# A hybrid decoder layer on one core: where squares, features and the last rows of a projection stand at a block change

## The chip, the cores and the metric

The kernel runs on one core of one Trainium2 chip. The metric is the device time of one execution in microseconds. Three executions of the kernel before gave 3461.42, 3449.73 and 3450.88 us, so the median is 3450.88 us. A lower time is better.

## What is computed

The reference is one layer of a decoder step, in float32. It takes a prompt of 2048 tokens (one sequence) and 8 x 8 sample tokens with a cache, 1024 channels wide.

```python
h = rmsnorm(x, norm_mix) * (1 + sc_m) + sh_m
proj = h @ w_in                      # 1024 x 3584: rq rk rv rg sq sk sv
ro = retention(rotary(rq), rotary(rk), rv)          # 4 heads, group norm, times silu(rg)
so = stick_breaking_attention(sq, sk, sv)           # 8 heads, causal, rms norm per head
x = x + g_m * (concat(ro, so) @ w_out)
h = rmsnorm(x, norm_ffn) * (1 + sc_f) + sh_f
a, b = h @ w_up_gate, h @ w_up_val   # 1024 x 2816 each
ff = (silu(causal_conv3(a)) * b) @ w_down
x = x + g_f * ff
y = rmsnorm(x, norm_final)
```

Scales, shifts and gates (`sc`, `sh`, `g`) come from a small product of the condition with `w_ada`. The outputs are `y` for prompt and sample, and the new keys, values, retention states and convolution states.

## The kernel before

**Precision.** Every large product is made of three matmuls: both operands are split into a high part (a rounded copy on ScalarE, L174) and a low part (the difference, on VectorE or GpSimd, L159), and high x high, high x low and low x high add up in one PSUM bank (`mm3`, L295 to L297). L159, L174 and L165 are lines of small helpers that record all element-wise operations, all splits and all DMAs, so in the profile one tells them apart by the names of the tiles.

**Tiles.** The prompt is cut into four blocks of 512 tokens (`g` = 0 to 3), each of four tiles of 128 tokens. The 64 sample tokens ride as a fifth tile with block 0 of the input projection and with block 3 of the output projection and the MLP. The features of the current block, the normalised and modulated rows turned so that channels lie across partitions, stand in two buffers `act0` and `act1` (channels 0 to 511 and 512 to 1023, high and low part). There is one set of them, so features of the next block overwrite those of the current one.

**How features are made.** Rows of a tile are squared on ScalarE with a running sum, GpSimd turns the sum into a factor (`rows_rstd`: add, scale, power), the rows are scaled by it, and `to_features` (L427) does the rest by halves: four transposes on TensorE into one `z` bank of PSUM (L401), modulation by two operations on VectorE for the first half of the channels or four on ScalarE (L413) for the second, the high part on ScalarE (L424), and the low part on VectorE or GpSimd.

**The input projection (`in_block`, L608).** For a block it computes the columns of `w_in` group by group: queries and keys with channels across partitions (weights stationary, `dense_pair`, `dense_fm`), and values and gate with tokens across partitions (`token_major`, L661: features stationary, four PSUM banks `d`, one per tile, a loop over eight k of 128 channels in pairs). In `token_major` the order is k by k over the tiles; only the last pair runs tile by tile (`by_tile`). After the loop come the weights of the next block's first columns (`next_weights`, loads and both splits), then `fin` for each tile, which empties its bank (`fin_rg`: sigmoid, two products, a store). RG is the last group in blocks 0 to 2. Ahead of it `look_ahead` loads and normalises the first three row tiles of the next block. The next block begins with `to_features` of all four tiles; the fourth is loaded and normalised there.

**Output projection and MLP.** `out_block` (L1205) adds the output projection to the rows in two halves of 512 columns. After the first half, tile by tile: a product with the gate on VectorE out of the PSUM bank into a buffer `hf`, an addition on GpSimd (`residual`), a square on ScalarE (L1240). After the second half, tile by tile: `residual`, square (L1243), factor, the scaling of both halves (L1245 and L1246). Then `to_features` for all tiles. `ffn_block` (L1269) runs over the 22 column tiles of the MLP in four parts (`PARTS`); each part computes gate and value columns, then adds its piece of the down product in two halves. In the last part, after the first half, come the residual, a square (L1390) and a product with the final norm's weights on GpSimd, tile by tile. Between the first and the second half of the last part the whole `out_block` of the next 512 tokens is run (`yield from after`), features included, and then the down product's second half, tile by tile, with the final norm (`finish`, L1347) behind it. The first gate columns of the next block are loaded and split just ahead of those residuals.

**What sets the order.** Each stage is a Python generator that yields an estimate of its TensorE time. `_weave` always advances the stream that is furthest behind its share, so input projection, decoding of the sample, retention and attention, and later the MLP and attention, alternate piece by piece. The source order that results is not yet that of the engines: the compiler plans each engine's queue by its own estimates, takes the source order as priority, and picks what it expects to be ready. On the chip each engine then runs its queue in order. Buffers are counted by tag: three `hf` in both phases, three `c` and two `a` for MLP blocks, six `whl` for split weights (a pair is one weight tile's high and low part), four `d` and three `z` banks in PSUM.

## Time and profile before

| | |
|---|---|
| median of three executions | 3450.88 us |
| the profiled execution's own time | 3453.42 us |
| its span, first to last instruction | 3451.7 us |
| mean granted TensorE clock | 0.982 |
| busy: TensorE / VectorE / ScalarE / GpSimd | 95% / 66% / 52% / 30% |
| DMA | 527.71 MB, 153 GB/s |

PE is the matrix engine (TensorE), PEld its weight loads, DVE VectorE, ACT ScalarE, POOL GpSimd, SP the engine whose queue issues the DMAs. Lines of a view name engine, source line, operation, the tiles as out<-in without buffer numbers, and times in microseconds or, for a mean of one, nanoseconds; a wait in brackets is the engine's idle time before an instruction and what ended it. PEclk is the share of the full clock that TensorE was granted. Input blocks 1, 2 and 3 begin at about 328, 627 and 914 us; features for the four MLP blocks are made from about 1285, 1850, 2430 and 2984 us; attention ends at 2885 us.

### The profile page before, as it was taken

To read this page: it belongs to the slowest core of one execution; us is meant where nothing else is said; L and a number is where in the kernel's file an instruction comes from. 1 tells how busy PE (TensorE), PEld (TensorE's weight loads), DVE (VectorE), ACT (ScalarE), POOL (GpSimd) and SP (SyncE) were. 2 spreads that over 40 slices of the span, in tenths; PEclk is the share of its full clock that TensorE was granted. 3 is DMA by queue.
4 is the path that set the end of the run, shared out by engine and by line. 5 is a ranking of instruction groups with operands and counts; after the bars stand their busy time and mean duration, and the time that the engine had idled before them with its cause. 6 is when DMAs were issued, how large, how long until landed. Compare 5 with 4: busy or idle time off the path is not lost. (4 is left out here: it accounts for less than half of the span.)

```text
span 3451.7 us, 49588 instructions
## 1 busy us (share of the span) xinstructions
PE 3287.4 (95%) x17111; PEld 2683.8 (78%) x17111; DVE 2288.9 (66%) x3258; ACT 1779.6 (52%) x3153; POOL 1018.7 (30%) x1898
## 2 busy tenths in 40 slices
PE   7998999999999989999998999999899999999998
PEld 5877777776677767877877788777677787799997
DVE  5466666665555567777777787876877775554545
ACT  5457566654544446555556555554655553433223
POOL 3012011101343233434334343333433323321113
PEclk8999999999999999999999999999999999999999
DMA  6766766666756773433454343335333334332221
GB/s 227 232 200 193 231 224 224 220 229 201 212 172 197 242 215 107 123 115 120 122 185 130 107 124 112 118 109 189 110 119 107 115 103 138 119 110 84 80 86 65
DMA packets 406232, 527.71 MB, mean 153 GB/s; under 512 B 27830, under 2 KB 244009, under 8 KB 405982
## 3 DMA queue, kind: packets, MB, share of 16 engines
q1 hardware_dynamic: 405982, 524.55, 48.4%
q8 instruction: 136, 2.23, 0.3%
q14 instruction: 114, 0.93, 0.1%
HBM read 442.47 MB, written 81.99 MB: 152 GB/s over the span
## 5 line engine op out<-in xcount | busy, mean ns | idle before, releaser
L159 DVE TENSOR_TENSOR whl<-raw,whl 128x1024 fp32r<-128x1024 f32 x456 | 572.9, 1260 | 557.5 <-ACT whl L174 552.2
L174 ACT CAST whl<-raw 128x1024 fp32r<-128x1024 f32 x456 | 477.1, 1050 | 901.7 <-PE d L296 636.4
L295 PE MATMUL d<-act,whl 128*128 128x512 f32 (+2 forms) x2016 | 740.3, 368 | 7.8 <-ACT act L424 7.0
L297 PE MATMUL d<-act,whl 128*128 128x512 f32 (+2 forms) x2016 | 736.0, 365 | 4.6 <-DVE whl L159 4.6
L296 PE MATMUL d<-act,whl 128*128 128x512 f32 (+2 forms) x2016 | 733.1, 364 | 3.1 <-POOL act L159 2.2
L295 PEld LDWEIGHTS d<-act,whl 128*128 128x128 f32 x2016 | 384.6, 191 | 67.9 <-ACT act L424 8.7
L297 PEld LDWEIGHTS d<-act,whl 128*128 128x128 f32 x2016 | 384.2, 191 | 64.8 <-DVE whl L159 5.9
L296 PEld LDWEIGHTS d<-act,whl 128*128 128x128 f32 x2016 | 385.4, 191 | 59.8 <-POOL act L159 2.6
L295 PE MATMUL d<-whl,ff 128*128 128x512 f32 x704 | 280.2, 398 | 0.0
L297 PE MATMUL d<-whl,ff 128*128 128x512 f32 x704 | 279.4, 397 | 0.0
L296 PE MATMUL d<-whl,ff 128*128 128x512 f32 x704 | 279.1, 396 | 0.0
L295 PE MATMUL d<-whl,act 128*128 128x512 f32 x640 | 258.0, 407 | 10.4 <-DVE hf L159 9.3
L296 PE MATMUL d<-whl,act 128*128 128x512 f32 x640 | 258.3, 404 | 0.1
L297 PE MATMUL d<-whl,act 128*128 128x512 f32 x640 | 257.1, 402 | 0.0
L1139 DVE TENSOR_TENSOR_SCAN aom<-aom,acy 128x512 f32<-128x512 f32 x192 | 251.6, 1310 | 3.6 <-ACT aom L1125 3.0
L159 DVE TENSOR_TENSOR abe<-abe,aom 128x512 f32<-128x512 f32 (+2 forms) x320 | 232.1, 725 | 27.0 <-POOL abe L1129 5.1
L1163 PE MATMUL acc<-ahl,avv 128*128 128x512 f32 (+3 forms) x640 | 226.4, 413 | 17.6 <-ACT ahl L174 9.9
L1125 ACT ACTIVATE aom<-z,nb 128x512 f32<-128x512 f32 (+2 forms) x320 | 201.4, 629 | 74.6 <-PE z L1122 58.1
L1122 PE MATMUL z<-akk,aq 128*128 128x512 f32 (+3 forms) x640 | 192.9, 377 | 12.0 <-DVE scd L159 5.8
L1126 ACT ACTIVATE abe<-z,bb 128x512 f32<-128x512 f32 (+2 forms) x320 | 200.1, 625 | 0.0
L159 DVE TENSOR_TENSOR ahl<-z,ahl 128x512 fp32r<-128x512 f32 (+1 forms) x320 | 191.4, 598 | 6.7 <-ACT ahl L174 6.4
L159 POOL TENSOR_TENSOR ff<-ff,hf 128x512 f32<-128x512 f32 (+1 forms) x101 | 159.4, 1600 | 105.3 <-DVE hf L159 91.5
(292 smaller groups left out, 6208.8 us busy)
## 6 DMA issues: line engine op xcount, KB each, us to landing
raw<-in_w_in SPq DMA_DIRECT2D x56, 1024.0 KB
raw<-in_w_up_gate SPq DMA_DIRECT2D x44, 1024.0 KB
raw<-in_w_up_val SPq DMA_DIRECT2D x44, 1024.0 KB
akk<-k SPq DMA_DIRECT2D x160, 256.0 KB
page<-in_cache_k_pages SPq DMA_DIRECT2D x128, 256.0 KB
page<-in_cache_v_pages SPq DMA_DIRECT2D x128, 256.0 KB
raw<-in_w_down SPq DMA_DIRECT2D x32, 1024.0 KB
raw<-in_w_ada SPq DMA_DIRECT2D x24, 1024.0 KB
```

The source lines that it names most:

```text
L159: eng.tensor_tensor(o, a, b, op)
L174: act.copy(hi, src)
L295: pe.matmul(ps, sh, mh, start=start, stop=False)
L296: pe.matmul(ps, sh, ml, start=False, stop=False)
L297: pe.matmul(ps, sl, mh, start=False, stop=stop)
L1122: pe.matmul(z[:, :n], qs[g, h][:, i * P : (i + 1) * P], kk[:, c, :n], start=c == 0, stop=c == 1)
L1125: act.activation(om[:, :n], z[:, :n], AF.Sigmoid, bias=nb[:, h : h + 1], scale=-SCALE)
L1126: act.activation(be[:, :n], z[:, :n], AF.Sigmoid, bias=bb[:, h : h + 1], scale=SCALE)
L1139: dve.tensor_tensor_scan(rv, rv, rv, init, ALU.mult, ALU.bypass)
L1163: pe.matmul(accs[0][:, cs], kv[u][1][:, kt, :], m[:, cs], start=(s == g and kt == 0 and c == 0), stop=(s == 0 and kt == NT - 1 and c == 1),)
```

## The change

It has two parts, both about the order of work where a block gives way to the next.

The MLP's part. A list `later` holds work that is to be put into the program some steps on; `tick` counts it down. In `out_block` the squares of the first half go in after two weight pairs of the second half, and in `ffn_block` the square and the product with the final norm's weights go in after the first weight pair of the next `out_block` (at once in the last block). The squares of the second half write their throw-away output to `hf` and follow all four residuals. `out_block` no longer makes the features; it returns a generator `features` that scales rows two tiles ahead. `ffn_block` takes one step of it ahead of the second half of the down product and one behind each tile's matmuls. For the first MLP block all of it runs at once, as before.

The input projection's part. In blocks 0 to 2 the RG columns go through `last_rows`: the first four k as before, the last four tile by tile, and behind each tile its `fin` and the features of the same tile of the next block. The first split of the next block's weights is put ahead of these tiles, the second behind them. `look_ahead` fetches all four row tiles, the fourth into a buffer of the tag `st`. The features at the start of a block and `next_weights` are gone.

```diff
     def in_rows(g, ip, i):
-        x = T(ip, [P, D], F32, "vst" if i == 2 else "xt")
+        x = T(ip, [P, D], F32, ("xt", "xt", "vst", "st")[i])
...
-        if g:
-            for i, o, n in tiles:
-                to_features(ahead.pop((g, i), None) or in_rows(g, ip, i), o, n, coef[0], coef[1], acts, ip)
...
+        def last_rows(col, fin):
+
+            pss = [pd() if i < NT else pz() for i, _, _ in tiles]
+            ws, nxt = [], None
+            for k0, (hi, lo) in w_tm(w_in, 0, KT, col):
+                if k0 >= KT - 4:
+                    ws.append((k0, hi, lo))
+                    continue
+                for k in range(k0, k0 + 2):
+                    for tile in tiles:
+                        tok_mm(
+                            pss[tile[0]], act_rows(k, tile, smp), (hi[:, k - k0, :], lo[:, k - k0, :]),
+                            k == 0, False,
+                        )
+                yield cost / 2
+            key = RQ if g + 1 == NB - 1 else SQ
+            nxt = w_fm(w_in, key)
+            first_in[g + 1, 0, key] = [next(nxt)]
+            for tile in tiles:
+                i, o, n = tile
+                for k0, hi, lo in ws:
+                    for k in range(k0, k0 + 2):
+                        tok_mm(
+                            pss[i], act_rows(k, tile, smp), (hi[:, k - k0, :], lo[:, k - k0, :]),
+                            False, k == KT - 1,
+                        )
+                fin(i, n, fold(pss[i], n, ip))
+                if i < NT:
+                    to_features(ahead.pop((g + 1, i)), o, n, coef[0], coef[1], acts, ip)
+                yield cost / len(tiles)
+            first_in[g + 1, 0, key] += list(nxt)
...
         def look_ahead():
-            if g + 1 < NB:
-                for i in range(3):
-                    ahead[(g + 1, i)] = in_rows(g + 1, ip, i)
+            for i in range(NT):
+                ahead[(g + 1, i)] = in_rows(g + 1, ip, i)
...
-            yield from token_major(RG, fin_rg, next_weights if g < NB - 1 else None)
+                yield from last_rows(RG, fin_rg)
+            else:
+                yield from token_major(RG, fin_rg)
...
+    later = []
+
+    def tick(n=1):
+
+        for e in later:
+            e[0] -= n
+        while later and later[0][0] <= 0:
+            later.pop(0)[1]()
...
+        def squares(i, half):
+            n = tiles[i][2]
+            junk = T(fp, [P, 512], F32, "hf")
+            act.activation(
+                junk[:n], x2[i][:n, half * 512 : half * 512 + 512], AF.Square, accum_out=ss[i][:n, half : half + 1]
+            )
...
                 yield cost / 2
-            cs = slice(half * 512, half * 512 + 512)
+                tick()
             for i, o, n in tiles:
                 residual(pss[i], gates[half][i == NT], x2[i], half, n, fp, dve if half else pool)
                 if half == 0:
-                    junk = T(fp, [P, 512], F32, "hf")
-                    act.activation(junk[:n], x2[i][:n, cs], AF.Square, accum_out=ss[i][:n, 0:1])
-                else:
-                    xa, xb = T(fp, [P, 512], F32, "c"), T(fp, [P, 512], F32, "a")
-                    act.activation(xa[:n], x2[i][:n, cs], AF.Square, accum_out=ss[i][:n, 1:2])
-                    r = rows_rstd(ss[i], n)
-                    act.activation(xa[:n], x2[i][:n, :512], AF.Copy, scale=r[:n, 0:1])
-                    dve.tensor_scalar(xb[:n], x2[i][:n, 512:], r[:n, 0:1], None, ALU.mult)
-                    xn.append((xa, xb))
+                    later.append([2, lambda i=i: squares(i, 0)])
+        tick(9)
+        rs = []
         for i, o, n in tiles:
-            to_features(xn[i], o, n, coef[2], coef[3], acts, fp)
-            yield 1.0
-        return x2
+            squares(i, 1)
+            rs.append(rows_rstd(ss[i], n))
+
+        def features():
+            xn = {}
+            for j in range(len(tiles) + 2):
+                if j >= 2:
+                    i, o, n = tiles[j - 2]
+                    to_features(xn[j - 2], o, n, coef[2], coef[3], acts, fp)
+                if j < len(tiles):
+                    i, o, n = tiles[j]
+                    xa, xb = xn[j] = T(fp, [P, 512], F32, "c"), T(fp, [P, 512], F32, "a")
+                    act.activation(xa[:n], x2[i][:n, :512], AF.Copy, scale=rs[i][:n, 0:1])
+                    dve.tensor_scalar(xb[:n], x2[i][:n, 512:], rs[i][:n, 0:1], None, ALU.mult)
+                if j >= 1:
+                    yield 1.0
+
+        return x2, features()
...
                 if last and half:
+                    feats = got[1] if got else iter(())
+                    next(feats, None)
                     wts = list(w_tm(w_dn, f0, f1 - f0, half * 512))
                     for tile in ordered:
                         for q0, w in wts:
                             for q in range(2):
                                 one(pss, tile, f0 + q0 + q, w, q)
                         yield cost * (f1 - f0) / 4 / len(tiles)
+                        next(feats, None)
+                    yield from feats
...
                         if last:
                             ss[i] = T(small, [P, 2], F32, f"os{i}")
-                            junk = T(fp, [P, 512], F32, "hf")
-                            act.activation(junk[:n], x2[i][:n, :512], AF.Square, accum_out=ss[i][:n, 0:1])
-                            tt(pool, x2[i][:n, :512], x2[i][:n, :512], nf[:n], ALU.mult)
+                            later.append([1, lambda i=i, n=n, nf=nf: first_half(i, n, nf)])
+                            if after is None:
+                                tick()
```

`first_half` holds the square and the product that stood there.

More of the change, by code (lines that the diff above doesn't have):

```diff
@@ L659, in k_rows, with token_major @@
                 sv(O["k_rows_sample"][:, j * P : (j + 1) * P], kr[:NS, :P])
-        def token_major(col, fin, then=None):
+        def token_major(col, fin):
             pss = [pd() if i < NT else pz() for i, _, _ in tiles]
@@ L669, in token_major @@
                 yield cost / 2
-            if then:
-                then()
             for i, o, n in tiles:
                 fin(i, n, fold(pss[i], n, ip))
+        def last_rows(col, fin):
[28 more added lines that the diff above has]
+            first_in[g + 1, 0, key] += list(nxt)
         def fin_v(i, n, ps):
@@ L719, in ret_qk @@
                         yield cost / 2
-        def next_weights():
-            col = RQ if g + 1 == NB - 1 else SQ
-            first_in[g + 1, 0, col] = list(w_fm(w_in, col))
         def look_ahead():
-            if g + 1 < NB:
-                for i in range(3):
-                    ahead[(g + 1, i)] = in_rows(g + 1, ip, i)
+            for i in range(NT):
+                ahead[(g + 1, i)] = in_rows(g + 1, ip, i)
         def stick():
             yield from sb_qk()
-            if g == NB - 1:
-                look_ahead()
             yield from token_major(SV, fin_v)
@@ L1346, in ffn_block, with first_half @@
                 conv_state(FT - 2, fp)
+            def first_half(i, n, nf):
+                junk = T(fp, [P, 512], F32, "hf")
+                act.activation(junk[:n], x2[i][:n, :512], AF.Square, accum_out=ss[i][:n, 0:1])
+                tt(pool, x2[i][:n, :512], x2[i][:n, :512], nf[:n], ALU.mult)
             def finish(i, o, n, nf, eng):
@@ L1490, in mlps @@
         def mlps():
-            st = yield from out_block(0, lambda: fp, fp, False)
+            st, feats = yield from out_block(0, lambda: fp, fp, False)
+            yield from feats
             for g in range(3):
                 nxt = out_block(g + 1, last_pool if g == 2 else lambda: fp, fp, g == 2)
-                st = yield from ffn_block(g, st, fp, False, nxt)
+                st = (yield from ffn_block(g, st, fp, False, nxt))[0]
             state.append(st)
```

1 line of the change is left out of this document (removed).

## The prediction

> **What bounds the kernel now.** I read the page first, then the waits of TensorE, then a table of windows around every place where one block of tokens hands over to the next, then single rows.
>
> ```profile
> span 3451.7 us, 49588 instructions
> PE 3287.4 (95%) x17111; PEld 2683.8 (78%) x17111; DVE 2288.9 (66%) x3258; ACT 1779.6 (52%) x3153; POOL 1018.7 (30%) x1898
> ```
>
> TensorE is busy for 95% of the span; the other engines are far from full. So the change can only pay with TensorE time that is lost now: 3451.7 - 3287.4 = 164 us of idle time, and what a lowered clock costs. The waits say at which steps a part of it lies:
>
> ```profile
> PE d L295 <- DVE hf L159: 10.1, 5, 5.8
> ...
> PE z L401 <- DVE hf L159: 8.4, 6, 2.5
> PE d L295 <- ACT act L424: 7.0, 4, 2.2
> ...
> PE z L401 <- ACT hf L413: 6.4, 6, 2.1
> ...
> PE z L401 <- ACT c L1245: 3.3, 4, 1.7
> ...
> PE d L296 <- POOL act L159: 2.2, 2, 1.2
> ...
> PE d L296 <- DVE act L159: 0.9, 1, 0.9
> ```
>
> (us in total, times, longest.) All seven belong to block changes: L401 is the transpose of new features, L424 and the `act` tiles are those features being split, L1245 scales the normalised rows, and `hf` in the first row is a residual product that must empty a PSUM bank. The windows, each around one change, give all idle time there; the last row is a stretch inside a block, for comparison.
>
> ```profile
> core 0: us, PE busy (x) PEld busy (x) DVE busy (x) ACT busy (x) POOL busy (x), PEclk, DMA share, GB/s
> 326.00:354.00 28.00, 20.90 (x124) 17.02 (x125) 18.71 (x24) 18.35 (x38) 10.06 (x9) 0.88 0.45 143
> 624.00:654.00 30.00, 23.47 (x152) 20.22 (x151) 20.73 (x28) 20.74 (x44) 9.41 (x11) 0.89 0.64 210
> 908.00:936.00 28.00, 21.45 (x127) 16.77 (x125) 16.34 (x31) 17.13 (x39) 14.34 (x22) 0.88 0.74 214
> 1280.00:1306.00 26.00, 16.99 (x75) 13.01 (x74) 20.93 (x31) 15.42 (x34) 11.77 (x26) 0.70 0.46 135
> 1843.00:1873.00 30.00, 24.78 (x133) 18.71 (x132) 27.14 (x40) 24.18 (x52) 13.80 (x25) 1.00 0.24 70
> 2424.00:2458.00 34.00, 28.10 (x146) 21.15 (x144) 28.64 (x41) 24.02 (x53) 17.63 (x27) 1.00 0.23 67
> 2980.00:3010.00 30.00, 22.88 (x111) 17.21 (x110) 24.36 (x47) 20.95 (x45) 12.54 (x19) 0.94 0.13 38
> 1783.00:1790.00 7.00, 6.04 (x29) 4.64 (x28) 6.19 (x7) 3.69 (x8) 4.26 (x4) 1.00 0.99 303
> 1814.00:1822.00 8.00, 6.57 (x31) 5.01 (x30) 4.89 (x6) 4.53 (x10) 4.20 (x5) 1.00 0.30 106
> 2354.00:2376.00 22.00, 16.19 (x63) 12.41 (x63) 11.27 (x15) 8.73 (x17) 13.52 (x12) 0.84 0.51 173
> 2929.00:2934.00 5.00, 3.92 (x18) 2.86 (x17) 1.14 (x2) 0.72 (x2) 4.17 (x4) 1.00 0.24 96
> 1910.00:1940.00 30.00, 30.00 (x141) 23.61 (x140) 25.16 (x30) 18.16 (x30) 9.97 (x17) 1.00 0.51 158
> ```
>
> Window less PE busy: the three input-block changes (rows 1 to 3) hold 7.10 + 6.53 + 6.55 = 20.2 us of idle time; the four places where MLP features are made (rows 4 to 7) 9.01 + 5.22 + 5.90 + 7.12 = 27.3 us; the four turns from a first half of 512 columns to what follows it (rows 8 to 11) 0.96 + 1.43 + 5.81 + 1.08 = 9.3 us. Together 56.8 us is in reach of the change, and no more than that but for the clock.
>
> One thing matters for all that follows: the engines do not run in the order of the source.
>
> ```profile
> 2986.78 0.39 PE L296 MATMUL d<-whl,ff 128*128 128x512 f32 x1
> 2987.01 0.40 PE L297 MATMUL d<-whl,ff 128*128 128x512 f32 x1
> 2988.92 0.66 PE L401 MATMUL z<-con,c 128*128 128x128 f32 x4 [1.51 <-DVE hf L159]
> ```
>
> Down matmuls (`d<-whl,ff`, one every 0.23 us) already stand between the transposes of features that the source puts wholly ahead of them. A planner in the compiler orders each engine by the times it expects, with the source order as priority; the chip then waits, here 1.51 us, where the expectation was too good. So a move in the source moves priorities, and part of what it asks for may be there already.
>
> **The change part by part.**
>
> *Squares later (first halves).* Now each tile's residual row goes through one chain:
>
> ```profile
> 2926.67 1.30 POOL L159 TENSOR_TENSOR ff<-ff,hf 128x512 f32<-128x512 f32 x1 [13.82 <-DVE hf L159]
> 2928.81 1.29 POOL L159 TENSOR_TENSOR ff<-ff,gp 128x512 f32<-128x512 f32 x1 [0.83 <-ACT hf L1390]
> 2930.05 1.30 POOL L159 TENSOR_TENSOR ff<-ff,hf 128x512 f32<-128x512 f32 x1
> ```
> ```profile
> 2928.01 0.63 ACT L1390 ACTIVATE hf<-ff 128x512 f32<-128x512 f32 x1 [3.27 <-POOL ff L159]
> ```
>
> From one tile's add on POOL to the next 2930.05 - 2926.67 = 3.38 us pass: add, square on ACT, product on POOL. The square's throw-away output shares the three `hf` buffers with the residual products, so the product of tile 3, which frees the fourth PSUM bank, stands behind the square of tile 1, which ends 3.38 + 1.30 + 0.63 us or more after the first add starts. With the squares behind, it stands behind the first add alone, 1.30 us. What this costs TensorE at the worst turn:
>
> ```profile
> 2369.46 0.80 PE L295 MATMUL d<-whl,act 128*128 128x512 f32 x1 [5.81 <-DVE hf L159]
> 2370.06 0.63 PE L296 MATMUL d<-whl,act 128*128 128x512 f32 x1
> 2370.48 0.63 PE L297 MATMUL d<-whl,act 128*128 128x512 f32 x1
> ```
>
> Of 9.3 us I take 8 as gone and leave 1.3, one POOL add that comes late. After the wait matmuls start 0.42 us apart instead of 0.23, and the granted clock of that window is 0.84: 22 x 0.16 = 3.5 us of clock. I take 2 of it. Sum 10; bounds 0 (the planner finds other work for that place on DVE) and 9.3 + 3.5 = 12.8. The work itself only moves: four adds in a row hold POOL 4 x 1.30 = 5.2 us, and attention's small POOL copies queue behind that; TensorE has the next half's matmuls as cover, and without it 5.2 - 3.4 = 1.8 us a turn would show.
>
> The Trainium skill, "TensorE: Matmul & The Clock Gate", Part 1, says that the array falls to half its rate after an idle window of about 3.4 us. By that the wait of 5.81 us agrees with what follows it, but the input changes, whose longest wait in the rows above is 2.5 us, should keep a full clock; the measured 0.88 there differs, and the measurement decides. By the rule alone the clock's 3 us in the next part would fall away and the sum would be 25 us instead of 28.
>
> *The input block's last rows by tile.* Now the gate columns' last k-pair runs by tile, then come the four fins, both splits of the next weights and all features. With the change the last four k run by tile, 12 matmuls x 0.23 = 2.8 us each, with that tile's transposes behind them, so tile 0's features get three tiles, 8.3 us, instead of 3 x 6 x 0.23 = 4.1 us; the fourth row tile is loaded and normalised with the others instead of at the change. What a tile's features need on each engine:
>
> ```profile
> L413 ACT ACTIVATE hf<-z,coef,coef 128x128 f32<-128x128 f32 x112 | 43.9, 458 | 15.1 <-PE z L401 6.0 <-POOL act L159 5.3 <-POOL hf L159 1.3
> L159 POOL TENSOR_TENSOR act<-hf,act 128x512 fp32r<-128x512 f32 x28 | 41.5, 1481 | 62.4 <-ACT act L424 62.1 <-DVE hf L159 0.4
> L424 ACT CAST act<-hf 128x512 fp32r<-128x512 f32 (+1 forms) x58 | 34.7, 616 | 7.7 <-DVE hf L159 7.4
> L174 ACT CAST whl<-raw 128x1024 fp32r<-128x1024 f32 x456 | 477.1, 1050 | 901.7 <-PE d L296 636.4 <-PE z L304 117.3 <-PE z L296 83.8
> L159 DVE TENSOR_TENSOR whl<-raw,whl 128x1024 fp32r<-128x1024 f32 x456 | 572.9, 1260 | 557.5 <-ACT whl L174 552.2
> ```
>
> On ACT 4 x 0.46 + 2 x 0.62 = 3.1 us, then 1.48 us on POOL: 4.6 us from transpose to the last low part, with DVE's share for the first half of the channels beside it. Tiles 0 and 1 are ready before the last matmul of RG; the next block opens with 2 x 24 matmuls of 256 columns on those two alone, half of 0.23 us each, 5.5 us, which hides tile 3. So the waits on `act` go, but for the one of the first MLP block (its window's own row):
>
> ```profile
> PE d L295 <- ACT act L424: 0.7, 1, 0.7
> ```
>
> That is 7.0 + 2.2 + 0.9 - 0.7 = 9.4 us. The transposes' own waits do not go by themselves: they now stand in front of RG matmuls instead of in front of the next block. The rest of the windows' 20.2 us, 10.8, is shared with decoding and attention; I take 2 of it. Clock: 28 x 0.12 + 30 x 0.11 + 28 x 0.12 = 10.0 us, part of which falls on idle time; I take 3. Sum 14. Upper bound 20.2 + 10.0 = 30; the lower one is below zero, priced in the second rival.
>
> Added: the second split of the next block's weights goes from ahead of the fins to behind the last tile, because its buffers are those of RG's weights. ACT 1.05 and DVE 1.26 follow the last RG matmul; the first weights' 24 matmuls, 2.8 us, hide them. I charge 2 us for the three changes; without cover it is 3 x 2.3 = 6.9. The moved load of the fourth row tile and the store queue on SP wait for nobody here: DMA share 0.45 to 0.74 in those windows.
>
> *Features between down tiles.* All second-half squares come first, in `hf` buffers rather than in those of the scaled rows, then rows are scaled two tiles ahead, and each tile's transposes rank behind that tile's 12 down matmuls. So the waits for scaled rows (3.3 us) go. The planner mixed these before; what remains is ACT:
>
> ```profile
> L1245 ACT ACTIVATE c<-ff,rs_b 128x512 f32<-128x512 f32 (+1 forms) x5 | 3.6, 724 | 4.1 <-POOL rs_b L159 4.1
> L1243 ACT ACTIVATE c<-ff 128x512 f32<-128x512 f32 (+1 forms) x5 | 3.1, 622 | 3.4 <-DVE ff L159 3.4
> ```
>
> In 2981:3008 ACT waits 4.1 us for the row factors from POOL and has little slack else (20.95 of 30 us busy in the window), so the last change can win about that 4.1 at most. The last tile's features, 3.1 us on ACT, now stand ahead of the next gate's splits, which can eat some of it. The first MLP block has no down matmuls to put between (9.01 us): I take nothing there. Waits of 3.3 and about 3 of the rest: 6. Bounds: minus 3 x 3.1 = -9, and 27.3.
>
> Sum: 10 + 14 + 6 - 2 = 28 us. The profiled execution took 3453.42 us, its span 3451.7 and 1.7 around it; that is 2.5 above the runs' median of 3450.88. So 3425.4 for such an execution and **3423** for the median.
>
> **The rivals.**
> 1. *The planner has it already.* Transposes and down matmuls alternate before the change; if its order was limited by the same ACT and POOL chains everywhere, only the bank waits go: 10 us, 3441. For it: DVE is busy for 27.14 of 30 us and ACT for 24.18 in 1843:1873. Against: the input features cannot start earlier without the change.
> 2. *Slower: transposes stall the matmuls behind them.* TensorE runs in order. 24 groups of four transposes in three input changes and 26 in three MLP changes now have cheap work behind them. L401's waits on `hf` average (8.4 + 6.4) / 12 = 1.23 us. If all 50 groups wait that long, 62 us stand against the 18 of today (8.4 + 6.4 + 3.3) and the 19 that go elsewhere (9.4 + 10): 25 us slower, 3476. It decides from a mean of 37 / 50 = 0.74 us a group. For it: the sample's accumulator keeps one of three `z` banks through the first input change. Against: today's 18 us come from 16 waits in 58 groups now.
> 3. *The clock.* If the short pauses inside the last rows held the clock at half, the 3 x 4 x 12 RG matmuls of 0.23 us would take 33 us more: 3423 + 33 = 3456. The windows' 0.88 with waits below 2.6 us speaks for it; 1.00 at 1843:1873 with 5.2 us of short waits against it. The Trainium skill's same page, "A second HAM failure mode: psum-queue depth-cycling", describes such micro-idling between groups; nothing here shows it beyond these rows.
> 4. *More goes.* If most idle time of the windows goes with its clock, 50 us: 3401.
>
> **How the numbers follow.** A measurement of this kernel can tell about 0.5%, 17 us. The forecast has 0.55, rival 1 0.20, rival 2 0.09, rival 3 0.04, rival 4 0.12. One tenth of the forecast's share falls short of 17 us. Faster: 0.50 + 0.12 = 0.62; within: 0.05 + 0.20 + 0.04 = 0.29; slower 0.09. The forecast's own range is 3405 to 3440; with rival 1 and half of rival 4 it is 3398 to 3450, which leaves out some 0.19.
>
> **What would show it.** Right: no 5.8 us row of `d` L295 on DVE `hf`; the waits on `act` L424 near the first MLP block's 0.7; a clock near 1 at the input changes; RG matmuls and L401 in turn. Wrong: L401's waits above 18 us in total (rival 2), clock below 0.88 (rival 3), MLP windows as idle as now (rival 1), or a wait for `whl` in the next block's first weights.

## The result and the profile after

Four executions of the changed kernel took 3421.25 to 3429.12 us, median 3424.15; the kernel before, run beside it, had a median of 3454.84. The ratio is 0.9912, with a 95% interval of 0.9895 to 0.9928: 25 to 36 us faster. The profiled execution took 3422.1 us. Two of the executions further down, one of x1 (5712 us) and one of x7 (16170 us), were far slower than the rest; they stand in the medians but not in the ratios. First the page of the changed kernel:

```profile
span 3420.4 us, 49521 instructions
PE 3273.5 (96%) x17111; PEld 2676.8 (78%) x17111; DVE 2287.6 (67%) x3258; ACT 1772.8 (52%) x3153; POOL 1029.1 (30%) x1898
```

The work is the same; idle time of TensorE fell from 164 to 146.9 us and its busy time by 13.9. The same matmuls in less busy time point to the clock, and the granted clock agrees: it was 0.982 before and 0.986 after, so 0.018 of 3451.7 us, 62 us, were not granted before and 0.014 of 3420.4 us, 48 us, after. TensorE's waits at block changes:

```profile
PE d L295 <- ACT whl L174: 5.5, 3, 4.4
PE z L401 <- ACT hf L413: 4.5, 3, 1.8
PE z L401 <- ACT c L1293: 4.0, 2, 2.3
PE z L295 <- ACT act L424: 3.6, 1, 3.6
PE z L401 <- DVE hf L159: 3.6, 4, 1.4
...
PE d L295 <- ACT act L424: 0.9, 2, 0.6
```

The bank wait of 5.8 us is gone and `act` L424 costs the `d` matmuls 0.9 instead of 7.0. Two rows have grown. The last MLP block's first gate matmul, behind the last tile's features, waited 1.8 us for `act` before and waits 3.6 now, in the direction of the prediction's ACT bound for that change. The waits of `d` for split weights on ScalarE (`whl` L174) were 1.1 us in total and are 5.5; one of them, 4.4 us, is new. The windows, shifted with the work (not all as long as those before), in the order of the prediction:

```profile
304.00:332.00 28.00, 26.00 (x145) 20.32 (x145) 24.69 (x35) 20.82 (x45) 10.80 (x9) 1.00 0.68 224
600.00:632.00 32.00, 29.86 (x181) 24.60 (x180) 27.25 (x38) 25.20 (x51) 10.45 (x10) 1.00 0.70 234
886.00:926.00 40.00, 33.66 (x211) 27.02 (x210) 28.00 (x49) 22.11 (x47) 18.44 (x29) 0.96 0.75 225
1270.00:1296.00 26.00, 19.55 (x108) 16.78 (x107) 20.18 (x28) 20.25 (x45) 13.72 (x26) 0.74 0.29 85
1824.00:1854.00 30.00, 25.43 (x143) 20.21 (x143) 25.79 (x40) 25.36 (x54) 14.39 (x28) 1.00 0.31 86
2394.00:2424.00 30.00, 24.51 (x130) 19.30 (x129) 27.63 (x39) 25.49 (x54) 16.44 (x28) 0.98 0.32 96
2950.00:2980.00 30.00, 23.62 (x118) 18.64 (x116) 24.35 (x49) 20.77 (x45) 10.11 (x19) 0.87 0.11 36
1764.00:1771.00 7.00, 7.00 (x34) 5.65 (x33) 5.49 (x7) 3.83 (x10) 5.82 (x6) 1.00 0.92 273
1794.00:1802.00 8.00, 7.53 (x37) 5.84 (x36) 7.20 (x8) 7.28 (x16) 5.85 (x6) 1.00 0.45 153
2332.00:2345.00 13.00, 13.00 (x64) 9.98 (x63) 10.35 (x11) 8.10 (x17) 12.92 (x10) 1.00 0.89 289
2893.00:2915.00 22.00, 17.61 (x70) 13.37 (x69) 3.83 (x5) 5.82 (x11) 9.05 (x8) 0.91 0.88 305
```

Window less busy time: input changes 2.00 + 2.14 + 6.34 = 10.5 us (20.2 before) with clocks of 1.00, 1.00 and 0.96 (0.88, 0.89, 0.88); MLP features 22.9 (27.3); three of the four turns 0.5 together. The fourth, the last block's, holds 4.39 us, nearly all of it the new wait. So the sum came out near the forecast while something was lost that the forecast did not have. The queue of SP, in the changed kernel, shows where it began:

```profile
2895.64 0.32 SPq L165 DMA_DIRECT2D gp<-gp  x1
...
2897.75 1.97 SPq L165 DMA_DIRECT2D ff<-in_x_prompt  x4
...
2900.82 1.14 SPq L165 DMA_DIRECT2D raw<-in_w_out  x2
```
```profile
2912.23 1.22 PE L295 MATMUL d<-whl,act 128*128 128x512 f32 x2 [4.36 <-ACT whl L174]
...
2914.51 0.63 PE L296 MATMUL d<-whl,act 128*128 128x512 f32 x1
2914.94 0.63 PE L297 MATMUL d<-whl,act 128*128 128x512 f32 x1
```

The second load of `w_out` is issued behind a gate load (`gp`, which had to wait for a buffer that a residual product frees) and five row loads; its split then comes late, TensorE waits 4.36 us, and the matmuls after that run 0.43 us apart instead of 0.23.

### The profile page after: what moved, and what is told of

Its sections match the earlier page's. It is cut to its first block, busy times and chain, and to the rows that moved or that the text cites. A ratio compares the mean times of both kernels' runs of the same rounds, so it can differ in the third digit from the quotient of the medians.

```text
span 3420.4 us, 49521 instructions
## 1 busy us (share of the span) xinstructions
PE 3273.5 (96%) x17111; PEld 2676.8 (78%) x17111; DVE 2287.6 (67%) x3258; ACT 1772.8 (52%) x3153; POOL 1029.1 (30%) x1898
## 4 chain that ended last, share of the span: by engine, by line
PE 45%; DVE 2%; POOL 1%; ACT 1%; issue 1%; DMA 1%; SPq 0%; POOLq 0%; DVEq 0%; ACTq 0%
PE d L295 11%; PE d L296 11%; PE d L297 11%; PE acc L1185 3%; PE z L1144 2%; PE z L1173 2%; PE z L297 1%; PE z L296 1%; PE z L295 1%; DVE whl L159 1%; DVE hf L159 1%; DVE aom L1161 0%; POOL ff L159 0%; ACT whl L174 0%; PE z L304 0%
## 5 line engine op out<-in xcount | busy, mean ns | idle before, releaser
L174 ACT CAST whl<-raw 128x1024 fp32r<-128x1024 f32 x456 | 477.2, 1050 | 940.9 <-PE d L296 661.7
L296 PE MATMUL d<-whl,ff 128*128 128x512 f32 x704 | 278.9, 396 | 0.0
L1343 DVE SCALAR_TENSOR_TENSOR c<-a,vecs,c 128x512 f32<-128x512 f32 x176 | 133.3, 759 | 81.8 <-ACT c L1340 47.2
```

The lines of the kernel that those rows point to most:

```text
L174: act.copy(hi, src)
L296: pe.matmul(ps, sh, ml, start=False, stop=False)
L1343: dve.scalar_tensor_tensor(c[:, :TB], a[:, j : j + TB], cw(j), c[:, :TB], ALU.mult, ALU.add)
```

## The experiments

The change has three parts: **A**, squares of first halves later; **B**, the input block's last rows tile by tile; **C**, MLP features between down tiles. Each kernel below was timed in rounds with the kernel before on its chip. From each trace I also took the start of the first matmul of some groups: the input stage reaches to the first matmul of the last input columns (SV of block 3), the rest from there to the end; "attention's lead" is the time from attention's last matmul to the last part of block 2's down product; a "turn" is from the first matmul of the first half of `out_block` to that of the second half.

| kernel | ratio to before, 95% | input stage | rest | attention's lead | turn, block 2 | turn, block 3 |
|---|---|---|---|---|---|---|
| before | 1 | 1173.1 | 2278.6 | 32.8 | 40.2 | 28.2 |
| changed: A, B, C | 0.9912 (0.9895 to 0.9928) | 1158.6 | 2261.8 | 24.4 | 31.8 | 33.5 |
| x1: B | 0.9977 (0.9967 to 0.9986) | 1160.3 | 2279.6 | 32.8 | 40.0 | 31.2 |
| x2: A | 0.9954 (0.9937 to 0.9971) | 1168.1 | 2262.1 | 32.8 | 30.3 | 27.3 |
| x3: C | 0.9999 (0.9986 to 1.0011) | 1166.0 | 2281.1 | 24.5 | 39.1 | 36.8 |
| x4: A, C | 0.9958 (0.9941 to 0.9974) | 1168.4 | 2262.2 | 24.5 | 31.7 | 35.1 |
| x8: A, B | 0.9928 (0.9914 to 0.9942) | 1161.5 | 2262.4 | 32.8 | 30.3 | 26.9 |
| x6: features last | 0.9959 (0.9944 to 0.9973) | 1175.4 | 2261.9 | 24.5 | 31.8 | 33.9 |
| x7: buffer | 0.9960 (0.9945 to 0.9974) | 1173.6 | 2272.8 | 32.8 | 37.4 | 27.5 |
| x11: buffer, product | 0.9966 (0.9950 to 0.9982) | 1168.2 | 2267.4 | 32.8 | 35.9 | 26.4 |
| x12: product | 0.9998 (0.9983 to 1.0013) | 1169.1 | 2276.2 | 32.8 | 38.8 | 28.4 |
| x5: loads late | 0.9917 (0.9902 to 0.9931) | 1161.9 | 2265.9 | 24.5 | 31.8 | 26.1 |
| x10: last loads late | 0.9894 (0.9871 to 0.9918) | 1155.5 | 2254.9 | 24.5 | 31.8 | 26.1 |
| x9: C, last loads late | 0.9972 (0.9958 to 0.9987) | 1171.8 | 2274.5 | 24.5 | 39.1 | 27.5 |

The input stage varies by itself: in the eight kernels with the old input part it took 1166.0 to 1173.6 us, mean 1169.8. Without A, and with the rest as before, the rest took 2276.2 to 2279.6.

### One part alone

x1, **B** alone: the input block as changed, everything behind it as before.

```diff
-            yield from token_major(RG, fin_rg, next_weights if g < NB - 1 else None)
+                yield from last_rows(RG, fin_rg)
```

> Only the input projection's part of the change. My sum: 12 us faster than the kernel before (14 for the features, 2 charged for the late weights), and idle time in the three input changes down from 20.2 us to about 8, as in the changed kernel. If the gain of the whole came from the MLP's part alone, this one is within 3 us of before.

Measured 3444.23 us against 3453.52, ratio 0.9977, 5 to 11 us faster. The five kernels that carry the changed part had input stages of 1155.5 to 1161.9 us, mean 1159.6, against 1169.8: 10 us. B wins about 8 to 10. What it wins is not mainly idle time. The whole input stage of the kernel before and of the changed one:

```profile
0.00:1173.00 1173.00, 1084.93 (x5907) 863.50 (x5908) 704.83 (x1168) 636.29 (x1171) 248.02 (x513) 0.97 0.66 213
```
```profile
0.00:1158.00 1158.00, 1075.52 (x5904) 856.16 (x5904) 700.28 (x1168) 632.15 (x1171) 250.36 (x512) 0.98 0.67 216
```

TensorE is idle for 88.1 and 82.5 us. Single traces differ by as much, so here are the means of all, by each kernel's own end of the stage: 85.0 us in the eight kernels with the old input part (81.4 to 88.1) and 81.9 in the five with the new one (78.6 to 84.3). Of the 9.7 us of idle time that went from the three changes, about 3 are left over the stage. The busy time of the same matmuls falls from a mean of 1084.8 (1082.1 to 1087.3) to 1077.6 (1072.4 to 1083.3), by 7. That is the clock, 0.97 and 0.98 in the two windows.

x2, **A** alone.

```diff
-                    act.activation(junk[:n], x2[i][:n, cs], AF.Square, accum_out=ss[i][:n, 0:1])
+                    later.append([2, lambda i=i: squares(i, 0)])
...
-                            tt(pool, x2[i][:n, :512], x2[i][:n, :512], nf[:n], ALU.mult)
+                            later.append([1, lambda i=i, n=n, nf=nf: first_half(i, n, nf)])
```

> Only the squares of the first halves are moved (out_block's first half, and the square and product after the last part's first half). My sum: 10 us faster, the 5.8 us wait of d L295 on DVE hf gone. Rival, that the whole gain is input rows: 0. Rival, that the w_out weights of the last block now come too late, since the loads did not become faster: 4 to 7 us of the 10 are given back at the last change, so 3 to 6 faster.

Measured 3434.1, ratio 0.9954, 10 to 22 us faster. The five kernels with A and the loads in their old place had 2261.8 to 2262.4 us for the rest, 16.0 below the mean of 2278.1 in the three with neither A nor C nor the buffer's change. So A is worth 16, not 10. The turn of block 2 gives 9.9 of it. The next largest piece is block 1's turn. There, the waits of the kernel before and then, for the same 272 matmuls, its window and that of x2:

```profile
PE d L295 <- DVE hf L159: 2.4, 2, 1.4
PE acc L1163 <- ACT ahl L174: 1.5, 1, 1.5
PE acc L1163 <- DVE ahl L159: 1.4, 1, 1.4
```
```profile
1784.00:1848.00 64.00, 58.67 (x272) 46.39 (x271) 41.42 (x55) 31.04 (x60) 24.86 (x42) 1.00 0.54 164
```
```profile
1779.00:1838.00 59.00, 57.51 (x272) 46.42 (x271) 44.98 (x53) 30.80 (x60) 28.52 (x42) 1.00 0.58 177
```

5 us less. 3.8 of it is idle time: the two bank waits (`d`), 2.4, and attention's wait for `ahl` on VectorE, 1.4, at 1801 us, between the windows that the prediction looked at. For the whole rest of the kernel, before and then x2:

```profile
1173.00:3451.00 2278.00, 2202.43 (x11207) 1820.28 (x11204) 1584.07 (x2090) 1143.27 (x1983) 770.64 (x1386) 0.99 0.40 122
```
```profile
1168.00:3430.00 2262.00, 2196.28 (x11207) 1816.42 (x11204) 1591.89 (x2090) 1142.02 (x1983) 778.67 (x1386) 0.99 0.40 123
```

In this pair A takes away 75.6 - 65.7 = 9.9 us of idle time and 6.2 of busy time. By the means of the three kernels without A and the five with it (by each kernel's own end of the input stage) it is 12.4 us of idle time, 77.74 to 65.36, and 3.7 of busy time, 2200.4 to 2196.7. The busy part is the clock; how the 16 us divide is known to 2 or 3 us.

x3, **C** alone.

```diff
-                    xn.append((xa, xb))
-        for i, o, n in tiles:
-            to_features(xn[i], o, n, coef[2], coef[3], acts, fp)
-            yield 1.0
-        return x2
+        return x2, features()
...
+                        next(feats, None)
```

> Only the MLP features between the down tiles, with the second halves' squares ahead of them; first halves' squares stay where they were. My sum: 6 us faster. Rival, that the compiler's planner had interleaved them already: within 2 us of before.

Measured 3451.57, ratio 0.9999: nothing. The stretch from the second half of block 0's `out_block` to the first down matmul, which holds the first MLP block's features, is 2.9 us shorter, against the forecast of none, but block 1's turn is 5.9 us longer and block 3's 8.5. There, at block 3's turn, the trace of x3 has

```profile
PE d L295 <- ACT whl L174: 6.2, 1, 6.2
```

x4, **A and C**, the input part as before (both edits above).

> The whole MLP part without the input projection's part. My sum: 16 us faster (10 and 6). If the parts share waits, less than the sum of the two measured apart. If the late w_out load of the last change belongs to the MLP part, a wait of d L295 for ACT whl of over 3 us is here as well.

Measured 3436.71, ratio 0.9958. With A beside it, C's long turn of block 1 is gone (29.6 us), the one of block 3 is not (35.1).

x8, **A and B**, features made in `out_block` as before: the edits of x1 and x2.

> The change without its feature part: squares of the first halves later, and the input block's last rows by tile; MLP features are made in out_block as before. Theory: the feature part wins some 8 us at the block changes and gives as much back at the last change, where it makes the w_out load late; so without it the time is that of the changed kernel within 3 us, 3426 (8 + 16.5 below the kernel before by the parts' own runs would be 3429), the turn out3h0 to out3h1 takes about 27 us and the first MLP block's stretch 146 instead of 143.7. Rival: the parts need each other, and the features' part is worth 6 us or more beside the other two: 3432 or more.

Measured 3427.15, ratio 0.9928. Its interval overlaps that of the whole change, so C adds nothing that these runs can tell from zero (3 us by the medians, 0.6 by the rest of the traces).

### Where C's gain went

x5: the changed kernel, with the gate and row loads behind the first weights of `w_out`.

```diff
+        def rows():
+            gates.extend(load_g(0, half, fp, samp and xpool) for half in range(2))
+            for i, o, n in tiles:
...
+                if half == 0 and k0 == 4:
+                    rows()
```

> The changed kernel, with one thing moved: the loads of the gate rows and of the block's rows in out_block go into the program behind the second pair of the first half's weights instead of ahead of the first. Theory: in the changed kernel attention ends only 24.4 us ahead of the last block's turn instead of 32.8, and a load of w_out stands on SP behind a gate load that waits for an hf buffer; that gives the 4.36 us wait of d on ACT whl L174 and the slow matmuls behind it. Then the wait goes, out3h0 to out3h1 falls from 33.5 to about 27 to 28 us, and the time is 5 to 7 us below the changed kernel: 3418. Rival 1: the load is late because the transfers themselves share the DMA engines with attention's last ones, so its place in the queue does not matter: 3424, and the wait stays above 3 us. Rival 2: the rows now come late and the residuals wait for them in other blocks: 3428 or more, with waits on DMA ff at the turns.

Measured 3425.16, ratio 0.9917: no gain as a whole, and two results in one. The turn of block 3 fell by 7.4 us to 26.1, which rules out rival 1. But the turn of block 0 rose from 40.1 to 46.5 and that of block 1 from 30.0 to 34.4. That is the loss that rival 2 named, but not its sign: no engine that computes waits for the row loads (`ff` on DMA) in the trace of x5, and how the late loads lengthen these two turns was not followed.

x10: the same for the last block only.

```diff
+        if not samp:
+            rows()
...
+                if samp and half == 0 and k0 == 4:
+                    rows()
```

> The changed kernel with the gate and row loads behind the first w_out weights in the last block's out_block only. With the loads late in every block, the turn out3h0 to out3h1 fell from 33.5 to 26.1 us, while out0h0 to out0h1 rose from 40.1 to 46.5 and out1h0 to out1h1 from 30.0 to 34.4. Theory: the late w_out load costs the change 7.4 us at the last change, and the rows came late only in the first two blocks. Then both early turns keep 40.1 and 30.0, the last has 26.1, and the time is 3424.2 - 7.4 = 3417. Rival: the loss at the early turns had another cause (a changed order further on), or the gain does not add up: 3421 or more.

Measured 3417.56, ratio 0.9894: 7 below the changed kernel by the medians (the intervals overlap), 6.9 by the rest of the traces, as expected; the early turns stayed at 40.7 and 29.6. Block 3's turn separates the kernels with C cleanly: 33.5 to 36.8 us in the four with the loads early, 26.1 to 27.5 in the three with them late. SP's queue in x10, and the last turn's window:

```profile
2890.49 0.42 SPq L165 DMA_DIRECT2D raw<-in_w_out  x1
...
2893.49 0.32 SPq L165 DMA_DIRECT2D gp<-gp  x1
...
2894.37 2.01 SPq L165 DMA_DIRECT2D ff<-in_x_prompt  x4
```
```profile
2893.00:2915.00 22.00, 22.00 (x96) 17.72 (x95) 3.52 (x4) 6.33 (x12) 7.38 (x7) 1.00 0.88 296
```

96 matmuls instead of 70 in the same 22 us (block 3's `out_block` begins at 2892.5 here and at 2894.7 in the changed kernel), with the DMA engines as busy (0.88 both times). The weights came in time because of their place in the queue, not because there was less to carry.

x9: C alone with that one load order.

```diff
+        return x2, features()
...
+                if samp and half == 0 and k0 == 4:
+                    rows()
```

> The kernel before with the feature part alone (features between the down tiles), and in the last block the gate and row loads behind the first w_out weights. The feature part alone gave 3451.6 against 3453.5, nothing that can be told. Theory: it wins about 8 us and gives as much back at the last change, where the turn out3h0 to out3h1 took 36.8 us; with the loads moved that turn takes about 28 and the time is 3443, ratio 0.9975. Rival: the planner had the features spread already, so there is nothing to uncover: 3449 or more, the turn above 34.

Measured 3445.83, ratio 0.9972, 4 to 15 us faster, with the turn at 27.5: C has a gain of its own, which the late load hid. With A and B beside it, it is 2262.4 - 2254.9 = 7.5 us (x8 against x10), one trace each. The idle time behind the input stage agrees: 71.5 us in x9 against the mean of 77.7 without A and C, and 60.1 in x10 against 66.7 in x8, 6.2 and 6.6 us less. The late loads without C were not run. At block 3's turn they could add little there, since x8 with early loads has 26.9 us and x10 26.1; elsewhere it is not known.

### What makes A's gain

x7: the kernel before, with only the throw-away output of the first-half squares in another buffer.

```diff
-                            junk = T(fp, [P, 512], F32, "hf")
+                            junk = T(fp, [P, 512], F32, "c")
```

> The kernel before, its order untouched; only the throw-away output of the two first-half squares (L1240 and L1390) goes into a buffer of the tag c instead of hf. Theory: the bank waits at the turns come from the squares holding hf buffers that the residual products need; then the 5.81 us wait of d on DVE hf goes and with it most of the 16 us that the squares' move alone won: 3440. Rival: the waits come from the place in the order, since the product on GpSimd stands between the adds and behind the square whatever buffer that writes; then the wait shrinks little and the time is within 3 us of the kernel before, 3450.

Measured 3441.56, ratio 0.9960, 9 to 19 us faster; by the rest of the trace 6. The bank wait is gone, so the shared buffer caused it, directly or through the planner, whose order also changes at the turns. Block 1's turn is as short as with all of A (28.8 us; 28.7 in x2, 31.9 before). Block 2's is still long. Here are 25 us from the start of `out_block` in block 2, for before, x7, and x2:

```profile
2359.00:2384.00 25.00, 19.19 (x75) 15.07 (x75) 13.40 (x15) 11.74 (x21) 10.93 (x13) 0.86 0.59 180
```
```profile
2357.00:2382.00 25.00, 22.59 (x89) 17.20 (x88) 17.27 (x17) 12.41 (x22) 12.41 (x14) 0.86 0.65 197
```
```profile
2349.00:2374.00 25.00, 25.00 (x115) 20.04 (x116) 19.09 (x20) 14.27 (x26) 14.13 (x13) 1.00 0.73 213
```

75, 89 and 115 matmuls. GpSimd's queue, x7 and then x2, shows one thing that differs:

```profile
2358.38 1.30 POOL L159 TENSOR_TENSOR ff<-ff,gp 128x512 f32<-128x512 f32 x1
2359.64 2.28 POOL L159 TENSOR_TENSOR ff<-ff,hf 128x512 f32<-128x512 f32 x1
2361.86 1.12 POOL L1136 COPY aom<-acy 128x1 f32<-128x1 f32 x1
```
```profile
2344.75 6.41 POOL L159 TENSOR_TENSOR ff<-ff,hf 128x512 f32<-128x512 f32 x4 [0.42 <-DVE hf L159]
2351.11 1.11 POOL L1136 COPY aom<-acy 128x1 f32<-128x1 f32 x1
```

Attention's copy comes 5.6 us after the first `w_out` matmul in x7 (2356.28) and 2.2 after it in x2 (2348.91); in x2 the four adds stand in a row and the products with the norm's weights behind them. ScalarE's queue, again x7 and then x2, shows another:

```profile
2357.19 0.63 ACT L1390 ACTIVATE c<-ff 128x512 f32<-128x512 f32 x1 [2.63 <-POOL ff L159]
...
2358.76 0.57 ACT L174 CAST ahl<-z 128x512 fp32r<-128x512 f32 x1
```
```profile
2348.19 0.58 ACT L174 CAST ahl<-z 128x512 fp32r<-128x512 f32 x1
```

In x7 a square holds ScalarE for 2.63 us until GpSimd's add is done, and attention's split `ahl` behind it starts 2.5 us after the first `w_out` matmul; in x2 the split is ahead of the squares and starts 0.7 us before that matmul.

x12 and x11 move only the products later, without and with the other buffer.

```diff
-                            tt(pool, x2[i][:n, :512], x2[i][:n, :512], nf[:n], ALU.mult)
+                            later.append(
+                                lambda i=i, n=n, nf=nf: tt(pool, x2[i][:n, :512], x2[i][:n, :512], nf[:n], ALU.mult)
+                            )
```

> The kernel before, but only the four products with the final norm's weights are put behind the first weight pair of the next out_block; the squares stay and write to hf. Theory of two causes: the add of one tile now stands next to the add of the tile before, so the chain of 3.38 us a tile shrinks to about 1.3 and the bank wait with it although the buffer is shared: most of the gain is here too, the turn out2h0 to out2h1 at 32 to 34 us and the time at 3441. Rival: the shared buffer alone decides: the wait of d on DVE hf stays above 4 us, the turn above 38, the time at 3449 or more.

> The kernel before, but the throw-away output of the first-half squares goes into a buffer of the tag c, and the four products with the final norm's weights on GpSimd go into the program behind the first weight pair of the next out_block; the squares stay where they are. With the buffer alone, the wait of 5.8 us was gone, but the turn out2h0 to out2h1 still took 37.4 us instead of 40.2 (30.2 with the squares' part whole): attention's matmuls waited 1.4 and 0.8 us there and the 21 matmuls behind took 7.4 us instead of 5.1. Theory: two causes, the shared buffer and the products that hold GpSimd ahead of attention's small copies. Then this kernel has out2h0 to out2h1 near 30 to 32 us and nearly all of the squares' part: 3439, 14 below the kernel before. Rival: the squares on ScalarE between attention's splits are what holds attention up: the turn stays above 36, the time at 3444 or more.

Measured 3451.72 (0.9998) and 3441.35 (0.9966). They look like the rivals' numbers (x12) or lie between theory and rival (x11), and mean something else: the queues of matmuls, weight loads, VectorE, ScalarE and GpSimd hold the same instructions in the same order as those of the kernel before (x12) and of x7 (x11). Presumably the planner had nothing else ready for GpSimd at that place, so a later position in the source moved nothing. So the two runs test neither theory nor rival; they are repetitions. They show what a difference is worth here: medians that agree within 2 us, but profiled spans 6.4 and 10.8 us apart, 2.4 and 5.4 of it behind the input stage. So 5 us in one trace prove nothing; the 16 of A and the 0 of C beside it stand in five traces within 0.6 us, and the buffer alone is worth 6 to 11 us by the two traces of its order and 12 to 14 by the two ratios: between a third and most of A's 16. Whether the rest comes from the products' place on GpSimd or from the squares' place on ScalarE is open: the timelines show both, and neither was tried by itself.

### What makes B's gain

x6: the changed kernel, with all features behind the last tile's rows.

```diff
-                if i < NT:
-                    to_features(ahead.pop((g + 1, i)), o, n, coef[0], coef[1], acts, ip)
                 yield cost / len(tiles)
+            for i, o, n in TILES:
+                to_features(ahead.pop((g + 1, i)), o, n, coef[0], coef[1], acts, ip)
```

> The changed kernel, but in last_rows all features stand behind the last tile's rows instead of each behind its own tile; loads, splits and the order of the rows stay as changed. Theory: what the input part wins (8 us by the kernel with this part alone) comes from features being made under the next tile's matmuls, so most of it goes: the three input windows idle 6 us more, and the time is 6 to 8 us above the changed kernel, 3431. Rival: the gain comes from the fourth row tile being loaded and normalised ahead and from the four last k by tile, which this kernel keeps, and the compiler's order pulls the features forward by itself: within 2 us of the changed kernel, 3424.

Measured 3439.02: not 7 but 15 us above the changed kernel, and with an input stage of 1175.4 us, 5.6 above the mean without B. The ratio, 0.9959, is that of x4 (0.9958), which has the same MLP part and the old input part. So features behind their own tile's matmuls are all of B's gain; last rows by tile with the features at the end win nothing, and whether they lose anything these runs do not show (the longest input stage with the old part was 1173.6). The transposes at the first input change, in the changed kernel and in x6:

```profile
L401 PE MATMUL z<-con,xt x16: 270/272/327, 308.9 to 314.8; 128*128 128x128 f32 x16
...
L401 PE MATMUL z<-con,st x8: 271/272/273, 325.3 to 327.2; 128*128 128x128 f32 x8
```
```profile
335.07 0.66 PE L401 MATMUL z<-con,vst 128*128 128x128 f32 x4 [1.31 <-DVE hf L159]
338.67 1.97 PE L401 MATMUL z<-con,st 128*128 128x128 f32 x8 [2.95 <-DVE hf L159]
340.29 0.78 PE L295 MATMUL d<-act,whl 128*128 128x256 f32 x2
```

Changed: spread over 18 us among RG matmuls. x6: at the end, with waits of 1.31 and 2.95 us in the open, and the next block's first matmul at 340.29 instead of 332.43, though RG began a little earlier (277.5, 278.9).

## Why the prediction was right, and where its terms were wrong

The total was right (28 us forecast, 30 measured, 25 to 36); its terms were mis-sized, and that the errors cancelled was luck. By the traces the parts are worth 16, 10 and about 0 us where the forecast had 10, 12 and 6. In the profiled runs the idle time fell by 17.4 us and the busy time by 13.9, where the forecast had 23 of waits and 5 of clock.

- **Squares later, forecast 10, measured 16**, above the upper bound of 12.8. At block 2's turn the reading held: 5.8 us of wait and 3.5 of clock, 9.9 measured. Over the kernels' means the waits were 12.4 where I took 8, and clock was 3.7 where I took 2 (9.9 and 6.2 in the one pair before and x2). The step that failed is the bound: it was made from windows of 5 to 22 us at the turns, and at block 1 a wait of attention between two windows went too. The note that attention's copies queue behind the adds had the wrong sign at block 2's turn: by the timeline, adds in a row let those copies through sooner than adds with products between them. "With the squares behind, the product stands behind the first add alone" is borne out by x7 as far as the buffer goes: without the sharing, the bank wait goes.
- **Last rows by tile, forecast 14 - 2, measured 8 to 10.** The size is near, its make-up is not. The windows lost the 9.4 us of `act` waits nearly as forecast, and the 2 us charged for the late second split were not there: no wait for `whl` stands at any of the three changes. But for the 11.4 us forecast as waits about 3 came, and for the 3 forecast as clock about 7. The step "10 us of clock, part of which falls on idle time; I take 3" was too small, and idle time taken out of a window was counted as taken out of the span. Decoding shares this stage, and idle time came back outside the windows; which waits took it up was not followed.
- **Features between down tiles, forecast 6, measured 0 in the change and 7.5 with the last loads in another place.** The local size was nearly right (with 2.3 to 3.4 of it in the first MLP block, where the forecast took nothing). What failed was the question not asked: the prediction weighed queues on SP for the input part only. With C, attention's last matmul comes 24.5 us ahead of block 2's last down part, in every kernel with C, and 32.8 in every one without it; attention's result tiles, the gate and the row loads then stand in front of `w_out` on SP.
- **Rivals.** The first (the planner has it already) is wrong for the features, whose move paid where it was let, and exactly right for the products of x12, which moved nothing. The second (transposes stall what is behind them): L401's waits on `hf` and on scaled rows fell from 18 to 12 us, far below the deciding 37; its "wrong" sign, a wait for `whl`, did come, at another change and for another reason. The third (clock at half in the last rows) did not come: the windows have 1.00, 1.00 and 0.96. The fourth (50 us) did not come either: the windows still hold 38 of their 56.8 us.

## What to carry to other kernels

When a reorder makes one stream finish later relative to another, look at what that stream's end triggers: loads queued on one DMA-issuing engine stand behind whichever of them waits for a buffer, and weights that are needed first may have to be issued before rows that are needed last. Try it at each place: here it won 7.4 us at the last block's turn and lost 6.4 and 4.4 at the first two. A scratch output that nobody reads still occupies a buffer that others wait for. A line moved in the source is not an instruction moved in a queue; compare the queues before reading a time.

## What the runs showed of the hardware

Nearly half of the gain in the profiled pair, 13.9 of 31.3 us, is busy time, so clock. At the input changes the granted clock went from 0.88, 0.89 and 0.88 to 1.00, 1.00 and 0.96 when transposes were spread, though no wait there had been above 2.5 us. The kernels x7 and x11 have the same queues and, at block 2's turn, the same two waits, and yet the clock cost them differently. First x7, then x11:

```profile
2365.77 0.50 PE L1163 MATMUL acc<-ahl,avv 128*128 128x512 f32 x1 [1.42 <-ACT ahl L174]
...
2368.24 0.79 PE L1163 MATMUL acc<-ahl,avv 128*128 128x512 f32 x1 [0.80 <-DVE ahl L159]
```
```profile
2358.24 0.51 PE L1163 MATMUL acc<-ahl,avv 128*128 128x512 f32 x1 [1.42 <-ACT ahl L174]
2360.71 0.80 PE L1163 MATMUL acc<-ahl,avv 128*128 128x512 f32 x1 [0.80 <-DVE ahl L159]
```

Behind the second wait, 13 gaps between matmuls were 0.43 us in x7 and 5 in x11, nearly all others 0.23. The clock records in the two traces say the same: half rate for 6.83 us in x7 (from 2367.63) and for 3.41 us in x11 (from 2360.19). In all fourteen traces the recorded clock is half or full, nothing between, and it changes only on a grid of 3.41 us, whose phase against the span's start varies between the traces. The Trainium skill, "TensorE: Matmul & The Clock Gate", Part 1, says that the window in which activity is counted runs freely, so that the same program can meet it at another phase; the grids agree with that. Whether the phase explains these two runs is not shown: half rate began 1.86 us behind the end of the first wait in x7 and 1.95 in x11, nearly the same. The Trainium skill's figure, in the same Part 1, of about 3.4 us without work before the rate halves does not describe them: the longest wait here is 1.42 us, in a stretch with few matmuls.
